# A hybrid decoder step: where the sums of x are formed, which slots the state tiles use, and whose queue loads the first merged values

## The chip, the cores and the metric

The kernel runs on one core of a Trainium2 chip. The metric is the device time of one execution in microseconds (us); less is better. The core's engines work side by side and meet at semaphores: TensorE (PE in the profile; PEld is its weight load), VectorE (DVE), ScalarE (ACT), GpSimd (POOL) and SyncE (SP, which here only issues DMAs). Each engine takes its own instructions in order. An instruction that waits holds up all that stand behind it on its engine, and the same goes for DMA issues on a queue.

## What is computed

One layer of a decoder for 2048 prompt tokens and 64 sample tokens (8 sequences of 8), model width 1024. Cut to what matters:

```python
z = x @ w_in                                   # q, k, v, gates of both branches
o_att = swa(q, k, v, sink, rel_bias)           # sliding window attention, with a relative bias
o_gla, S = gla(gq, gk, gv, log_a, s0)          # gated linear attention, 4 heads, state S carried on
h_att = (o_att * silu(g_att)) @ w_pa
h_gla = (norm(o_gla) * silu(g_gla)) @ w_pg
merged = sigmoid(r_att) * h_att + sigmoid(r_gla) * h_gla
y = merged @ w_o
x = layer_norm(ALPHA * x + y, ln_g, ln_b)
```

The recurrent state of the samples (`s0`) is read, advanced and written back as an output.

## The kernel before

**Stages.** The program runs in four stages: attention (to about 350 us of the span), GLA head by head (352 to 1080 us, each head six chunks of 384, 384, 384, 384, 256 and 320 tokens), the merge passes (four products, `w_pa`, `w_ra`, `w_rg`, `w_pg`, in 84 units; to 1660 us), and the output projection with the layer norm (to the end).

**Split values.** Every fp32 operand of a matmul is split in a high and a low part: ACT casts the high part (`CAST`, L112) and DVE, sometimes POOL, subtracts it (L113). A product is three matmuls: high by high, high by low, low by high (L182 to L184, L195 to L197, L1218 to L1220). So PE waits for an ACT cast and then a DVE or POOL subtraction of each new operand.

**Sums of x.** The merge passes use a scheme with seven products in place of eight: it multiplies sums and differences of blocks of the operands. `combine_x` forms four such values from two 128x704 rows of x, by four `tensor_tensor` of 128x352 on POOL (L855 to L858), loads the two rows on SP's queue (L853), and stores each result with a DMA of its own, also on SP's queue (L860). A list of 30 sums waits to be done: 6 of the attention's output (`ua_d` to `ac_d`), 12 of the input (`xT` to `xc_d`), 12 of the GLA's output (`ug_d` to `uc_d`). In GLA two of them are done at the start of each of the chunks 0, 1 and 2 of a head, 24 in all; six are left for the merge passes.

**Pools.** `wtile` gives a 128x1024 slot of a pool of 28. The weights' parts, the values `gv`, the rows x1 and x2 of the sums, the bias of the attention and `S0`, the samples' state, all turn in these slots, and the pools of the next stage lie in the same memory. At the end of a head `samp_b` advances `S0` (L836) and writes it out (L838, `o_ss<-S`): on SP, but in the last head on POOL's queue.

**Order.** PE's instructions are written out by hand. The other engines' order is made by a scheduler. `tc.issue_after(...)` holds an instruction of another engine behind a named one.

**Out of the merge stage.** `merge_sink` (L1096) forms merged values on DVE and SP stores them (`mg_d<-a`, L1099). `load_m` loads the first eight 128x384 tiles of them back (`xst<-mg_d`, L1168), ACT and DVE split them (`x`), and the projection's first matmuls (L195 to L197 with `woh`, `wol`) use them.

Of the kernel before, what the change touches and what calls it, by code (L numbers as in the profile page):

```python
# [21 lines left out]
P = 128  # L22
D = 1024
# [28 lines left out]
def kernel(ctx, tc, io):  # L52
# [19 lines left out]
    def wtile(dt=F32, name="w"):  # L72
        return sb.tile([P, D], dt, tag="w", name=name, bufs=28)

# [144 lines left out]

    st, hi, lo = sb.tile([P, D], F32, tag="wst", name="wst", bufs=2), wtile(F32R, "wh"), wtile(F32R, "wl")
# [88 lines left out]
    def setup2():  # L311
        flat = bs_d.rearrange("h q j -> h (q j)")
        for kv in range(2):
            b = wtile(name="bias").rearrange("p (g k) -> p g k", g=G)
            for g in range(G):
                f = flat[kv * G + g, 127:127 + P * (LB - 1)].rearrange("(q j) -> q j", j=LB - 1)
                nc.gpsimd.dma_start(b[:, g, :], f[:, :2 * W])
            st1["bias", kv] = b
# [470 lines left out]
    def samp_a(B):  # L789
# [20 lines left out]
        for bh in (0, 4):  # L810
            S0 = wtile(name="S0").rearrange("p (b v) -> p b v", b=4)
            nc.sync.dma_start(S0, io["state"][bh:bh + 4, B["h"]].rearrange("b k v -> k b v"))
            B["S0", bh] = S0
# [33 lines left out]

    def combine_x(new):
        src, dst, kh, k, s = combos.popleft()
        ts = slice(2 * s * MT, 2 * (s + 1) * MT)  # L850
        x1, x2 = new("x1")[:, :2 * MT], new("x2")[:, :2 * MT]
        for x_, k_ in ((x1, k), (x2, kh + k)):
            nc.sync.dma_start(x_, ug_d[k_ // 2][:, k_ % 2, ts] if src is None else src[:, k_, ts])  # L853
        t0, t1 = slice(0, MT), slice(MT, 2 * MT)
        nc.gpsimd.tensor_tensor(x2[:, t1], x2[:, t1], x1[:, t1], ALU.subtract)  # L855
        nc.gpsimd.tensor_tensor(x1[:, t1], x1[:, t1], x1[:, t0], ALU.subtract)
        nc.gpsimd.tensor_tensor(x1[:, t0], x1[:, t0], x2[:, t1], ALU.add)
        nc.gpsimd.tensor_tensor(x2[:, t0], x1[:, t0], x2[:, t0], ALU.subtract)  # L858
        for n_, x_, t in ((0, x1, t1), (1, x1, t0), (2, x2, t1), (3, x2, t0)):
            nc.sync.dma_start(dst[n_, :, s, k], x_[:, t])  # L860

# [22 lines left out]
    for h in range(GH):  # L884
        W2 = {}
        wcap(16 + 6 * h)
        for c, (t0, T) in enumerate(CHUNKS):
# [12 lines left out]
            gla_z(B)  # L900
            if c < 3:
                for _ in range(2):
                    combine_x(lambda n: wtile(name=n))
            wv = [wt2("v", 0), wt2("v", 1)]
# [24 lines left out]
            proj(ps[:, :T], wt2("k"), x, T)  # L929
            gla_k(B, ps[:, :T])  # L930
            if len(CHUNKS) - 4 < c < len(CHUNKS) - 1:
                wload()
# [7 lines left out]
            gla_q(B, ps[:, :T])  # L940
            tick()
            if end:
                chain(B)
# [43 lines left out]
    class Pass:  # L987
# [31 lines left out]
        def raw_x(self, i, s):  # L1019
# [7 lines left out]
            else:  # L1027
                d = [self.kept[{7: 2, 6: 1, 5: 0, 4: 3}[i]][:, s, :self.kh]]
            n = self.kh // len(d)
# [132 lines left out]

    def load_m(t, u, n, last=False):

        out = []
        for k in range(KT):
            st = ox.tile([P, TM], F32, tag="xst", name="xst", bufs=8)
            nc.sync.dma_start(st[:, :n + 32 * last], mg_d[t][:, k, u:u + n + 32 * last])  # L1168
            if last:
# [22 lines left out]
    for n, (q, i, s) in enumerate(units):  # L1192
        if n >= 2 * len(ORDER) * MS and n % 3 == 0 and combos:
            with tc.issue_after(pin["x"].ins), tc.issue_after(pin["p"].ins):
                combine_x(lambda t: mtile("xc", 2 * T, 5))
        if n >= 3 * len(ORDER) * MS and n % 4 == 0 and len(wo) < 4:
# [29 lines left out]
        if n == len(units) - 2:  # L1226

            xf, x, xr0 = load_m(1, 0, TM), [], []
    phase.close()
# [195 lines left out]
```

## Time and profile before

| what | value |
|---|---|
| median of 3 runs | 1871.84 us (1870.64 to 1873.26) |
| the profiled execution, its time | 1869.53 us |
| its span, first to last instruction | 1867.8 us |
| PE busy | 1818.6 us (97%) |
| DVE busy | 1252.3 us (67%) |
| ACT busy | 850.9 us (46%) |
| POOL busy | 513.0 us (27%) |
| mean granted TensorE clock | 0.988 |

The table is read from the top: an engine that is busy for 97% of the span is the bound, and the time that it isn't busy, 49.2 us, is what others make it wait for. A granted clock of 1.00 is 2.4 GHz; the other level is 1.2 GHz, and a mean between them says which part of a stretch ran at which. Time at the lower level counts as busy, so it does not show in PE's share.

### The profile page before, as it was taken

How to read it: one execution, taken by the hardware profiler on the slowest of the kernel's cores; microseconds unless marked ns; L12 is line 12 of the kernel's file. 1: busy time of each engine (PE TensorE's matmuls, PEld its weight loads, DVE VectorE, ACT ScalarE, POOL GpSimd, SP SyncE). 2: the span in 40 equal slices, each digit the busy share in tenths (PEclk: the TensorE clock that was granted, in tenths of full speed). 3: DMA queues.
4: the chain of work that ended last, by engine and by line, in shares of the span. 5: the costliest groups of instructions: out<-in, count | busy, mean ns of one | idle time of the engine just before them, and what ended most of it. 6: DMA issues, size and time to landing. Idle time of an engine off the chain costs nothing.

```text
span 1867.8 us, 32468 instructions
## 1 busy us (share of the span) xinstructions
PE 1818.6 (97%) x11683; PEld 1727.2 (92%) x11683; DVE 1252.3 (67%) x2566; ACT 850.9 (46%) x1947; POOL 513.0 (27%) x655
## 2 busy tenths in 40 slices
PE   8999999999999999999999989999999999999997
PEld 7989898899999999999999979999999999987886
DVE  6686688755675666657665659758656666956655
ACT  5444455545664664556455543444543543221110
POOL 3310111412134114211421124421255153631111
PEclk9999999999999999999999989999999999999999
DMA  7111003533365237514642179868887866895531
GB/s 240 53 55 38 27 32 123 178 129 104 108 212 182 81 104 234 178 57 140 203 134 73 42 248 313 278 200 275 292 318 259 299 217 244 282 310 187 157 117 40
DMA packets 200513, 315.84 MB, mean 169 GB/s; under 512 B 22413, under 2 KB 162149, under 8 KB 200336
## 3 DMA queue, kind: packets, MB, share of 16 engines
q1 hardware_dynamic: 194736, 306.19, 49.8%
q0 software_dynamic: 5616, 7.58, 1.5%
q8 instruction: 92, 1.51, 0.3%
q14 instruction: 69, 0.57, 0.1%
HBM read 228.52 MB, written 86.14 MB: 168 GB/s over the span
## 4 chain that ended last, share of the span: by engine, by line
PE 42%; DVE 4%; DMA 3%; POOL 2%; issue 1%; ACT 1%; SPq 0%; DVEq 0%; POOLq 0%; ACTq 0%
PE pa L1219 8%; PE pa L1218 8%; PE pa L1220 8%; PE pd L196 4%; PE pd L197 4%; PE pd L195 4%; PE pd L183 2%; PE pd L184 2%; PE pd L182 2%; DMA cs<-tt_d 1%; DVE xl L113 1%; DVE wl L113 0%; DVE fin L1096 0%; PE pa L750 0%; PE pa L751 0%
## 5 line engine op out<-in xcount | busy, mean ns | idle before, releaser
L182 PE MATMUL pd<-x,wh 128*128 128x384 f32 (+2 forms) x1248 | 410.5, 329 | 6.1 <-ACT x L112 5.9
L183 PE MATMUL pd<-x,wh 128*128 128x384 f32 (+2 forms) x1248 | 405.3, 325 | 0.4 <-POOL x L113 0.2
L184 PE MATMUL pd<-x,wl 128*128 128x384 f32 (+2 forms) x1248 | 404.7, 324 | 0.6 <-DVE wl L113 0.6
L1219 PE MATMUL pa<-xl,wh 128*128 128x352 f32 x1176 | 380.1, 323 | 9.8 <-DVE xl L113 9.4
L1218 PE MATMUL pa<-xh,wh 128*128 128x352 f32 x1176 | 381.7, 325 | 0.3 <-ACT wh L112 0.3
L1220 PE MATMUL pa<-xh,wl 128*128 128x352 f32 x1176 | 379.5, 323 | 0.0
L182 PEld LDWEIGHTS pd<-x,wh 128*128 128x128 f32 x1248 | 237.5, 190 | 16.0 <-issue 8.9
L183 PEld LDWEIGHTS pd<-x,wh 128*128 128x128 f32 x1248 | 237.5, 190 | 1.5 <-DVE x L113 1.1
L184 PEld LDWEIGHTS pd<-x,wl 128*128 128x128 f32 x1248 | 237.3, 190 | 1.0 <-DVE wl L113 1.0
L1219 PEld LDWEIGHTS pa<-xl,wh 128*128 128x128 f32 x1176 | 222.9, 190 | 12.4 <-DVE xl L113 12.4
L1218 PEld LDWEIGHTS pa<-xh,wh 128*128 128x128 f32 x1176 | 222.0, 189 | 1.1 <-ACT wh L112 0.4
L1220 PEld LDWEIGHTS pa<-xh,wl 128*128 128x128 f32 x1176 | 222.0, 189 | 0.0
L113 DVE TENSOR_TENSOR xl<-xs,xh 128x1408 fp32r<-128x1408 f32 x63 | 111.8, 1774 | 68.5 <-ACT xh L112 67.5
L195 PE MATMUL pd<-wh,x 128*128 128x256 f32 x512 | 149.6, 292 | 2.9 <-ACT x L112 2.7
L196 PE MATMUL pd<-wh,x 128*128 128x256 f32 x512 | 147.7, 289 | 2.7 <-DVE x L113 1.9
L197 PE MATMUL pd<-wl,x 128*128 128x256 f32 x512 | 145.7, 285 | 0.0
L112 ACT CAST x<-xst 128x384 fp32r<-128x384 f32 (+2 forms) x164 | 78.5, 485 | 140.2 <-PE pd L196 117.5
L112 ACT CAST xh<-xs 128x1408 fp32r<-128x1408 f32 x63 | 86.6, 1374 | 100.9 <-PE pa L1220 75.7
L742 POOL TENSOR_SCALAR sq<-sq 128x1 f32<-128x1 f32 (+1 forms) x68 | 18.3, 269 | 366.4 <-ACT ring L741 366.3
L195 PE MATMUL pd<-woh,x 128*128 128x512 f32 x256 | 102.6, 401 | 3.7 <-ACT x L112 3.7
L196 PEld LDWEIGHTS pd<-wh,x 128*128 128x128 f32 x512 | 98.9, 193 | 6.2 <-DVE x L113 5.7
L197 PE MATMUL pd<-wol,x 128*128 128x512 f32 x256 | 102.5, 400 | 0.6 <-DVE wol L113 0.6
(318 smaller groups left out, 3755.2 us busy)
## 6 DMA issues: line engine op xcount, KB each, us to landing
wst<-wt SPq DMA_DIRECT2D x33, 512.0 KB, 3.6
xs<-xc_d SPq DMA_DIRECT2D x24, 704.0 KB, 5.3
cs<-tt_d SPq DMA_DIRECT2D x48, 352.0 KB, 4.9
u<-xT SPq DMA_DIRECT2D x84, 192.0 KB, 3.8
xst<-xT SPq DMA_DIRECT2D x76, 192.0 KB, 2.7
xs<-xT SPq DMA_DIRECT2D x18, 704.0 KB, 6.1
ws<-w_ra SPq DMA_DIRECT2D x36, 256.0 KB, 4.3
ws<-w_rg SPq DMA_DIRECT2D x36, 256.0 KB, 4.6
```

The costliest lines, as they stand in the source:

```text
L112: pin["a"] = nc.scalar.copy(dst_h, src)
L113: i = eng.tensor_tensor(dst_l, src, dst_h.bitcast(F32), ALU.subtract)
L182: mm(ps, hi[:, s], xh[:, :T], start=(k == 0), stop=False)
L183: mm(ps, hi[:, s], xl[:, :T], start=False, stop=False)
L184: mm(ps, lo[:, s], xh[:, :T], start=False, stop=(k == n - 1))
L195: mm(ps, xh[:, xs], hi, start=(k == 0), stop=False)
L196: mm(ps, xl[:, xs], hi, start=False, stop=False)
L197: mm(ps, xh[:, xs], lo, start=False, stop=(k == KT - 1))
L742: nc.gpsimd.tensor_scalar(sq[:n], sq[:n], EPS, None, op0=ALU.add)
L1218: mm(ps, wh[:, ks], xh[:, ts], start=(k == 0), stop=False)
L1219: mm(ps, wh[:, ks], xl[:, ts], start=False, stop=False)
L1220: mm(ps, wl[:, ks], xh[:, ts], start=False, stop=(k == q.kh - 1))
```

## The change

The change has three parts.

1. **Slots.** The pool of 128x1024 slots has 26 in place of 28. Two slots of their own, with tag "s", lie at the bottom of the pool (`stile("first")` takes the place before anything else). The attention's bias and GLA's `S0` use them.
2. **Sums.** `combine_x` becomes `combine_load` and `combine_do`. In GLA the loads are written at the start of the chunk, and the four operations go to DVE: one sum behind `gla_k`, one behind `gla_q`, each held behind the instruction in `pin["d"]`. The chunks are 1, 2 and 3 of a head, not 0, 1 and 2. In the merge passes the operations stay on POOL. The four results are stored with two DMAs, not four, in another order of n, and the list of which result is kept where follows that.
3. **Queue.** The first `load_m` issues its eight loads on ACT's queue, not on SP's.

```diff
-        return sb.tile([P, D], dt, tag="w", name=name, bufs=28)
+        return sb.tile([P, D], dt, tag="w", name=name, bufs=26)
+    def stile(name):
+        return sb.tile([P, D], F32, tag="s", name=name, bufs=2)
...
+    stile("first")
...
-            b = wtile(name="bias").rearrange("p (g k) -> p g k", g=G)
+            b = stile("bias").rearrange("p (g k) -> p g k", g=G)
...
-            S0 = wtile(name="S0").rearrange("p (b v) -> p b v", b=4)
+            S0 = stile("S0").rearrange("p (b v) -> p b v", b=4)
...
-    def combine_x(new):
+    def combine_load(new):
         src, dst, kh, k, s = combos.popleft()
         ts = slice(2 * s * MT, 2 * (s + 1) * MT)
         x1, x2 = new("x1")[:, :2 * MT], new("x2")[:, :2 * MT]
         for x_, k_ in ((x1, k), (x2, kh + k)):
             nc.sync.dma_start(x_, ug_d[k_ // 2][:, k_ % 2, ts] if src is None else src[:, k_, ts])
+        return x1, x2, dst[:, :, s, k]
+
+    def combine_do(x1, x2, dst, eng):
+
         t0, t1 = slice(0, MT), slice(MT, 2 * MT)
-        nc.gpsimd.tensor_tensor(x2[:, t1], x2[:, t1], x1[:, t1], ALU.subtract)
-        nc.gpsimd.tensor_tensor(x1[:, t1], x1[:, t1], x1[:, t0], ALU.subtract)
-        nc.gpsimd.tensor_tensor(x1[:, t0], x1[:, t0], x2[:, t1], ALU.add)
-        nc.gpsimd.tensor_tensor(x2[:, t0], x1[:, t0], x2[:, t0], ALU.subtract)
-        for n_, x_, t in ((0, x1, t1), (1, x1, t0), (2, x2, t1), (3, x2, t0)):
-            nc.sync.dma_start(dst[n_, :, s, k], x_[:, t])
+        eng.tensor_tensor(x2[:, t1], x2[:, t1], x1[:, t1], ALU.subtract)
+        eng.tensor_tensor(x1[:, t1], x1[:, t1], x1[:, t0], ALU.subtract)
+        eng.tensor_tensor(x1[:, t0], x1[:, t0], x2[:, t1], ALU.add)
+        eng.tensor_tensor(x2[:, t0], x1[:, t0], x2[:, t0], ALU.subtract)
+        for n_, x_ in ((0, x1), (2, x2)):
+            nc.sync.dma_start(dst[n_:n_ + 2].rearrange("n p t -> p n t"), x_.rearrange("p (n t) -> p n t", n=2))
...
             gla_z(B)
-            if c < 3:
-                for _ in range(2):
-                    combine_x(lambda n: wtile(name=n))
+            sums = [combine_load(lambda n: wtile(name=n)) for _ in range(2 if c in (1, 2, 3) else 0)]
+
+            def combine():
+                if sums:
+                    with tc.issue_after(pin["d"].ins):
+                        combine_do(*sums.pop(0), nc.vector)
...
             gla_k(B, ps[:, :T])
+            combine()
...
             gla_q(B, ps[:, :T])
             tick()
+            combine()
...
-    def load_m(t, u, n, last=False):
+    def load_m(t, u, n, last=False, queue=nc.sync):
...
-            nc.sync.dma_start(st[:, :n + 32 * last], mg_d[t][:, k, u:u + n + 32 * last])
+            queue.dma_start(st[:, :n + 32 * last], mg_d[t][:, k, u:u + n + 32 * last])
...
-                combine_x(lambda t: mtile("xc", 2 * T, 5))
+                combine_do(*combine_load(lambda t: mtile("xc", 2 * T, 5)), nc.gpsimd)
...
-            xf, x, xr0 = load_m(1, 0, TM), [], []
+            xf, x, xr0 = load_m(1, 0, TM, queue=nc.scalar), [], []
```

PE's order is the same before and after. On the other engines the scheduler's order moves, at these three places above all.

On ACT, where the attention's last blocks overlap GLA's first chunk: `em`, `ek`, `dm` and `gb` are GLA's exponentials, `pT` is the transposed probabilities that PE's L417 waits for. Before:

```order
L386 ACTIVATE s,sm<-s,nm 128x256 x4
L388 ACTIVATE es<-es 128x4
L701 ACTIVATE em<-dm 128x384
L702 ACTIVATE ek<-ek 128x384
L703 ACTIVATE dm<-dm 128x384
L704 ACTIVATE gb<-gb 128x384
L112 CAST gv<-pd 128x256
L406 COPY pT<-pa 128x512
```

After:

```order
L390 ACTIVATE s,sm<-s,nm 128x256 x4
L392 ACTIVATE es<-es 128x4
L410 COPY pT<-pa 128x512
L705 ACTIVATE em<-dm 128x384
L706 ACTIVATE ek<-ek 128x384
L707 ACTIVATE dm<-dm 128x384
L708 ACTIVATE gb<-gb 128x384
L115 CAST gv<-pd 128x256
```

The copy of `pT` has moved from behind the four exponentials to ahead of them.

On DVE, in chunk 1 of the first head, from the parts of `ak` to the gates. Before:

```order
L113 TENSOR_TENSOR ak<-pa,ak 128x128
L715 TENSOR_TENSOR em<-pd,em 128x384
L715 TENSOR_TENSOR ek<-pd,ek 128x384
L767 SCALAR_TENSOR_TENSOR ring<-ring,e_4734,pa 128x256
L113 TENSOR_TENSOR st<-ring,st 128x256
```

After:

```order
L116 TENSOR_TENSOR ak<-pa,ak 128x128
L863 TENSOR_TENSOR x_5140<-x_5140,x_5139 128x352
L864 TENSOR_TENSOR x_5139<-x_5139 128x352
L865 TENSOR_TENSOR x_5139<-x_5139,x_5140 128x352
L866 TENSOR_TENSOR x_5140<-x_5139,x_5140 128x352
L719 TENSOR_TENSOR em<-pd,em 128x384
L719 TENSOR_TENSOR ek<-pd,ek 128x384
```

A sum of four instructions stands ahead of `em`; the chunk's second sum stands in the same way between a `st` and the `sg` of L784.

On SP's queue, in the first two chunks of the first head (`ua_d<-sil` stores the attention's last output, `u<-xT` loads the next chunk's x). Before:

```order
L853 DMA x_4749<-ua_d 128x704
L860 DMA ac_d<-x_4737 128x352
L860 DMA ac_d<-x_4736 128x352 x2
L860 DMA ac_d<-x_4737 128x352
L860 DMA ac_d<-x_4749 128x352
L860 DMA ac_d<-x_4748 128x352 x2
L860 DMA ac_d<-x_4749 128x352
L424 DMA ua_d<-sil 128x320 x4
L147 DMA u<-xT 128x384 x4
```

After:

```order
L857 DMA x_4718<-ua_d 128x704
L150 DMA u<-xT 128x384 x2
L428 DMA ua_d<-sil 128x320 x4
L150 DMA u<-xT 128x384 x2
L857 DMA x_5139<-ua_d 128x704
L857 DMA x_5140<-ua_d 128x704
L857 DMA x_5143<-ua_d 128x704
L868 DMA ac_d<-x_4713 128x2x352
```

The loads of x have moved from behind the sums' eight stores to ahead of them, and the next chunk's sums are loaded before this chunk's are stored.

At the end of the merge stage ACT's order now has the eight loads of `load_m` as two groups of four: one ahead of the last unit's `xh` (the high part of its operand), one behind it, and the eight casts `x<-xst` behind that.

## Rows read from the trace of the kernel before

**Rows 1.** PE's waits over the whole span: what waited for what, us in total, times, the longest.

```profile
PE pa L1219 <- DVE xl L113: 9.4, 5, 6.2
PE pd L195 <- ACT x L112: 6.5, 4, 3.7
```

**Rows 2.** Windows of the span (from:to, its length, then busy us of each engine, the granted clock, the DMA share and GB/s).

```profile
355.00:372.00 17.00, 13.70 (x73) 9.99 (x73) 14.77 (x27) 10.28 (x28) 9.93 (x10) 0.80 0.55 179
405.00:435.00 30.00, 27.46 (x168) 26.67 (x168) 11.72 (x31) 9.03 (x28) 17.32 (x22) 0.94 0.59 200
540.00:555.00 15.00, 13.81 (x104) 12.75 (x103) 11.66 (x24) 10.07 (x24) 4.59 (x6) 1.00 0.69 217
...
700.00:735.00 35.00, 33.08 (x228) 31.82 (x227) 26.08 (x68) 20.85 (x55) 11.06 (x15) 0.95 0.73 239
735.00:880.00 145.00, 144.96 (x1040) 143.00 (x1040) 91.37 (x231) 83.44 (x201) 33.98 (x60) 1.00 0.40 126
880.00:905.00 25.00, 23.47 (x170) 22.41 (x170) 17.84 (x39) 13.34 (x33) 10.38 (x13) 1.00 0.60 195
...
1064.00:1092.00 28.00, 19.50 (x122) 16.80 (x121) 15.63 (x50) 10.07 (x32) 7.29 (x15) 0.82 0.60 198
...
1655.00:1690.00 35.00, 30.62 (x130) 24.53 (x129) 18.67 (x31) 9.01 (x14) 6.75 (x8) 0.90 0.89 303
```

**Rows 3.** PE in order of time, where attention gives way to GLA (start, us, instruction, count, idle time before it and what ended that).

```profile
363.24 1.08 PE L417 MATMUL pa<-pT,vt 128*64 128x512 f32 x4 [1.42 <-ACT pT L406]
365.94 1.97 PE L417 MATMUL pa<-pT,vt 128*64 128x512 f32 x2 [1.62 <-DVE pT L404]
...
371.95 0.34 PE L197 MATMUL pd<-wl,x 128*128 128x256 f32 x1
```

**Rows 4.** ACT there: the copy behind the four exponentials (L701 to L704).

```profile
362.60 0.58 ACT L406 COPY pT<-pa 128x512 f32<-128x512 f32 x1
```

**Rows 5.** DVE in order of time there.

```profile
362.11 3.17 DVE L392 TENSOR_SCALAR s<-s,rd 128x256 f32<-128x256 f32 x4
365.20 0.68 DVE L404 COPY pT<-pa 128x512 f32<-128x512 f32 x1
```

**Rows 6.** POOL in order of time there: the first and the last of eight instructions of sums, back to back.

```profile
355.51 0.93 POOL L855 TENSOR_TENSOR x<-x,x 128x352 f32<-128x352 f32 x1
...
363.95 0.93 POOL L858 TENSOR_TENSOR x<-x,x 128x352 f32<-128x352 f32 x1
```

**Rows 7.** PE's longest wait in the second chunk of the first head.

```profile
421.61 0.39 PE L749 MATMUL pa<-st,qih 128*128 128x256 f32 x1 [2.26 <-ACT st L112]
```

**Rows 8.** ACT in order of time there.

```profile
418.20 1.00 ACT L112 CAST x<-u 128x384 fp32r<-128x384 f32 x2 [5.39 <-DMA u<-xT]
```

**Rows 9.** SP's queue there (start, time of the issues together, count).

```profile
403.87 7.42 SPq L860 DMA_DIRECT2D ac_d<-x  x8
411.38 1.86 SPq L424 DMA_DIRECT2D ua_d<-sil  x4
413.35 2.04 SPq L147 DMA_DIRECT2D u<-xT  x4
```

**Rows 10.** POOL there: the last of eight instructions of sums, back to back from 402.88.

```profile
409.99 0.95 POOL L858 TENSOR_TENSOR x<-x,x 128x352 f32<-128x352 f32 x1
```

**Rows 11.** PE in order of time where the merge passes begin.

```profile
1087.31 0.66 PE L1219 MATMUL pa<-xl,wh 128*128 128x352 f32 x1 [6.15 <-DVE xl L113]
...
1092.41 0.32 PE L1218 MATMUL pa<-xh,wh 128*128 128x352 f32 x1
```

**Rows 12.** DVE in order of time there.

```profile
1080.74 0.99 DVE L780 SCALAR_TENSOR_TENSOR sg<-pa,nw_h,sg 128x128 f32<-128x128 f32 x4
1086.36 0.89 DVE L113 TENSOR_TENSOR xl<-xc,xh 128x704 fp32r<-128x704 f32 x1 [4.63 <-DMA o_ss<-S]
```

**Rows 13.** POOL's last issue of the samples' state there.

```profile
1081.13 0.76 POOL L838 DMA_DIRECT2D o_ss<-S  x1 [1.09 <-DVE S L836]
```

**Rows 14.** PE where the output projection begins.

```profile
1664.01 0.80 PE L195 MATMUL pd<-woh,x 128*128 128x512 f32 x1 [3.74 <-ACT x L112]
...
1669.04 0.43 PE L197 MATMUL pd<-wol,x 128*128 128x512 f32 x1
```

**Rows 15.** SP's queue there.

```profile
1659.01 4.07 SPq L1168 DMA_DIRECT2D xst<-mg_d  x8
```

**Rows 16.** ACT there.

```profile
1649.43 1.37 ACT L112 CAST xh<-xs 128x1408 fp32r<-128x1408 f32 x1 [8.19 <-DMA xs<-uc_d]
1663.44 4.16 ACT L112 CAST x<-xst 128x384 fp32r<-128x384 f32 x8 [12.64 <-DMA xst<-mg_d]
```

**Rows 17.** Groups of instructions by line and shape: count, busy us, mean ns of one, idle time before them. A 128x352 operation on POOL and on DVE.

```profile
L855 POOL TENSOR_TENSOR x<-x,x 128x352 f32<-128x352 f32 x24 | 23.4, 975 | 54.3 <-DMA x<-ua_d 46.5 <-DMA x<-xT 4.9 <-DMA x<-ug_d 2.9
...
L1078 DVE TENSOR_TENSOR a<-a,pa 128x352 f32<-128x352 f32 x48 | 23.8, 515 | 5.9 <-PE pa L1220 5.8
```

**Rows 18.** DVE in order of time in the third chunk of the second head, a chunk in which PE waits for nothing.

```profile
624.33 0.56 DVE L715 TENSOR_TENSOR em<-pd,em 128x384 f32<-128x384 f32 x1 [1.63 <-PE pd L184]
...
626.22 0.43 DVE L113 TENSOR_TENSOR st<-ring,st 128x256 fp32r<-128x256 f32 x1 [0.47 <-ACT st L112]
...
635.24 0.61 DVE L780 SCALAR_TENSOR_TENSOR sg<-pa,nw_h,sg 128x128 f32<-128x128 f32 x2 [1.51 <-PE pa L777]
...
639.96 0.56 DVE L218 SCALAR_TENSOR_TENSOR sg<-th,pd 128x384 f32<-128x384 f32 x1 [1.15 <-ACT th L217]
```

More of the change, by code (lines that the diff above doesn't have):

```diff
@@ L1027, in raw_x @@
             else:
-                d = [self.kept[{7: 2, 6: 1, 5: 0, 4: 3}[i]][:, s, :self.kh]]
+                d = [self.kept[{6: 0, 5: 1, 4: 2, 7: 3}[i]][:, s, :self.kh]]
             n = self.kh // len(d)
```

## The prediction

> **What bounds the kernel now.** PE does. It is busy for 1818.6 of 1867.8 us, its instructions and their order stay as they are, so the change can only give back time in which PE waits or runs at the lower clock, or add to it. I read PE's waits first [rows 1]: the two longest entries are DVE's xl (9.4 us, one of them 6.2) and ACT's x (6.5 us, one of 3.7), a single stall each at a stage's border. Then I cut the span into windows [rows 2]. Undisturbed GLA loses nothing (144.96 busy of 145 us), so the losses sit in a few windows, and for each I read in order of time which engine came last. The other thing to see in a window is the granted clock: 0.80, 0.82, 0.90 and 0.94 mean that after the stall PE ran on at 1.2 GHz for some us. That loss is no idle time and comes on top.
>
> **The change part by part.** All times are of the profiled execution (1869.53 us, its span 1867.8), which is 2.31 us below the median of the runs shown; the sum is made on it, and the 2.31 is added at the end.
>
> (a) 355 to 372 us, attention into GLA: idle 17.00 - 13.70 = 3.3 us [rows 2]. PE waits 1.42 us for ACT's pT and 1.62 for DVE's, and then runs at half speed until 371.95 [rows 3]: from 365.94 that is 6.0 us, half of it lost, 3.0. At stake: 6.3. ACT's copy at 362.60 stands behind four exponentials of GLA [rows 4]. DVE's copy at 365.20 stands behind an L392 group that took 3.17 us [rows 5], all while POOL does eight instructions of sums from 355.51 to 364.88 [rows 6]. After the change no sum is done in chunk 0, and on ACT pT stands ahead of the exponentials. I take 5.0. Ends: 2.0 (ACT's wait and a part of the clock's loss) and 6.3.
>
> (b) 405 to 435, second chunk of the first head: idle 30.00 - 27.46 = 2.54, clock 0.94 of 30 us = 1.8 more [rows 2], 4.3 together. PE's 2.26 us for st [rows 7] go back to ACT, which sat 5.39 us for the load u<-xT [rows 8]. SP issued it at 413.35, behind eight stores of sums, 7.42 us [rows 9], that waited for POOL's sums, the last at 409.99 [rows 10]. Now the loads stand ahead of the stores, and there are four stores, not eight. I take all 4.3; ends 2.5 (the idle alone) and 4.3.
>
> (c, d, e) The other heads' starts: idle 15.00 - 13.81 = 1.2 at 540, 35.00 - 33.08 = 1.9 and 0.05 of 35 = 1.75 of clock at 700, 25.00 - 23.47 = 1.5 at 880 [rows 2]. All have sums of chunk 0 on POOL in the window, with their loads and stores on SP. These move to the chunks 1 to 3. 6.4 at stake. I take all of it; the low end is 1.9, if only the idle at 700 goes.
>
> (f) 1064 to 1092, the first merge unit. PE waits 6.15 us for xl and then runs at half speed until 1092.41 [rows 11], 5.1 us, of which 2.55 are lost. DVE had been free since 1081.73 and waited 4.63 us for the DMA o_ss<-S [rows 12], which POOL issued at 1081.13 [rows 13]: the xl tile lies where an S0 tile lay. With S0 in slots of its own, xl needs only its operand and its cast. DVE's sg (L780) then ends at 1081.73, and xl takes 0.89, so PE goes on at about 1082.6, 4.7 us earlier. I take 5.0, as a shorter stall should also leave some of the clock. Ends: 4.4, and 7.0 if PE never falls to the lower clock. DVE's next late partner would be a weight's part (wl) in a slot of the last stores, one unit later and off the path.
>
> (g) 1655 to 1690, the output projection: idle 35.00 - 30.62 = 4.38 [rows 2], with the half speed from 1664.01 to 1669.04 [rows 14], 2.5, in all 6.9. ACT's casts of x wait 12.64 us and end at 1667.6 [rows 16]; SP issues the loads only at 1659.01, in 4.07 us [rows 15], as they stand behind the last units' stores and loads on its queue. On ACT's queue they have no such neighbours: ACT sat idle 8.19 us ahead of the last xh [rows 16], so four loads go out in that gap and four right behind that cast, at 1650.8 to 1652.9. From issue to the first cast it took 1663.44 - 1659.01 = 4.4 us, so the last four can be cast from 1657.3, 0.52 each, and end at 1659.4, before PE asks at 1664.01 - 3.74 = 1660.27. I take 6.0, since waits for wol stay. Ends: 3.0 and 6.9.
>
> (h) Added on DVE: 24 sums of four 128x352 operations. On POOL one took 975 ns, on DVE the same shape takes 515 [rows 17], though there with one operand in PSUM: 4 x 0.515 = 2.06 us a sum, 24 x 2.06 = 49 us. DVE in a chunk of GLA is 63% busy (91.37 of 145) [rows 2]. In a chunk in which PE waits for nothing the gaps are [rows 18]: 1.63 us ahead of em, where the first sum goes, and 1.51 ahead of sg, where the second goes. Each is short by some 0.5 us (0.43 and 0.55). The next gaps, 0.47 ahead of st and 1.15 ahead of the second gate, take that up. So the cover is DVE's own idle time; without it the cost is 12 x 0.98 = 11.8 us. The range is 0 to 11.8. I take 3.0, near the lower end, because rows 18 are of a chunk that gets sums now.
>
> What costs nothing: POOL loses 96 operations, 96 x 0.975 = 94 us of work, which nobody asks for. S0's loads stand earlier on SP and wait there for the state's store; what stands behind them is x of the chunk after, wanted much later. The pool of 26 slots lost exactly the two that S0 or the bias took.
>
> Sum: 5.0 + 4.3 + 6.4 + 5.0 + 6.0 = 26.7, less 3.0 = 23.7. 1869.5 - 23.7 = 1845.8, and with 2.3, **1848.1 us**. By all high ends (30.9, nothing added) 1840.9; by all low ends (13.8 gained, 11.8 added) 1869.8.
>
> At (g) a rule speaks against my 6.0. The row shows 4.07 us of issue on SP and a last cast 7.3 us after PE asked for the first. The Trainium skill, "DMA: Bandwidth & Descriptors", section "Issuing engines are not separate DMA queues", says that DMAs from several engines run on the same 16 DMA engines and that spreading them saves only the issuing sequencer's time. By it (g) would be worth 4.1 at most, and the sum 1850. I keep 6.0, since what I count is that the loads leave SP's queue position, not that they run faster.
>
> **The rivals.**
>
> *The stalls come back in another coat.* At each head's start other things lie close behind: the cast of st, the ring on POOL's sq, the subtraction of x. If half of (a) to (g) returns, the gain is 13.4, less 3 = 10.4: 1861.5. For it: rows 2 show several small waits in each window. Against: the sums are the common part of all of them.
>
> *Only the issue time is saved at (g)*, by waits of ACT's queue for the last stores of merged values: 4.1 less what ACT's last xh loses behind four issues (4.07 / 2 = 2.0). Then 1852. For it: ACT works in order. Against: 8.19 us of idle time there.
>
> *The sums on DVE cost more than the stalls (slower).* DVE works in order. If a sum's row of x has not landed, or a sum is longer than its gap, everything behind it waits: em, the state's parts, the gate, the next chunk's x, and then PE. The point from which it decides: 26.7 / 24 = 1.1 us of PE's time for each sum. At 2.06, a whole sum on the path, it is 49.4 - 26.7 = 22.7 slower: 1895. For it: SP is in order too, one load of a pair has a slot that is free late, and the sums stand ahead of em. Against: the loads stand a chunk ahead of their sums, and rows 18 have gaps nearly as long as the sums.
>
> *The change doesn't do what it says*, as xl or pT waits for something as late as before: (f) or (a) alone is 5 us of the 23.7, so this ends between the first rival and the forecast, or within 0.2% if both fail and the sums cost their upper end.
>
> **How the numbers follow.** My forecast 0.62, half returned 0.17, issue time only 0.09, slower by DVE 0.07, nothing left of the gain 0.05. Faster by over 0.2% (3.7 us, about what a measurement of this kernel tells from no change) is the first three, 0.88; same 0.05; slower 0.07. The range 1840 to 1862 takes in the high ends and the first two rivals, and leaves out the last two cases and some of the error in the sum: 0.18.
>
> **What would show it.** In the trace of the changed kernel PE's wait for xl at the first merge unit should be under 2 us and ACT's x at the projection under 1. The windows at the five GLA starts should have a clock of 0.95 or more and idle times under 1 us, but for the first. DVE should have 49 us more, POOL 94 less, and PE's list of waits should have no new line at em, st, sg or x within chunks 1 to 3; such lines, 24 times over, would make the prediction wrong on the slow side. If xl is late again, look for what holds its tile.

## The result, and the profile after

The changed kernel takes 1844.84 us (median of 4 runs, 1843.05 to 1846.22) against 1871.24 (4 runs, 1866.16 to 1873.26): ratio 0.9862, 95% interval 0.984 to 0.9885, so 26.4 us less by the medians. The forecast was 1848.1 with 23.7 less on the trace; the two profiled executions differ by 23.3 (1869.53 and 1846.22).

PE's waits over the whole span, to be held against [rows 1]:

```profile
PE pa L1233 <- DVE xl L116: 7.6, 5, 2.6
PE pd L185 <- ACT x L115: 6.3, 3, 4.9
PE pa L1232 <- ACT xh L115: 2.3, 1, 2.3
PE pa L421 <- DVE pT L408: 1.1, 1, 1.1
```

ACT's x at the projection (L195 before, L198 now) has left the list. L185 was there before too, 5.9 us with a longest of 4.7: it is the start of the program. The longest wait for xl fell from 6.2 to 2.6 us, and a new line has come: xh, 2.3 us once.

The windows that answer to [rows 2] (same columns; each place lies earlier by what was won ahead of it):

```profile
350.00:370.00 20.00, 18.93 (x145) 17.00 (x145) 16.95 (x45) 18.10 (x52) 3.89 (x4) 1.00 0.46 141
394.00:426.00 32.00, 32.00 (x272) 31.68 (x271) 21.07 (x55) 16.44 (x41) 3.20 (x7) 1.00 0.61 206
527.00:545.00 18.00, 18.00 (x140) 17.59 (x140) 12.05 (x40) 13.12 (x34) 2.05 (x4) 1.00 0.56 168
685.00:720.00 35.00, 35.00 (x262) 34.59 (x261) 26.00 (x75) 23.30 (x59) 5.65 (x10) 1.00 0.54 166
715.00:860.00 145.00, 144.96 (x1039) 143.00 (x1038) 103.41 (x266) 83.13 (x202) 20.11 (x44) 1.00 0.47 150
860.00:890.00 30.00, 30.00 (x226) 29.61 (x225) 21.18 (x62) 20.72 (x56) 2.95 (x7) 1.00 0.46 137
1045.00:1075.00 30.00, 26.24 (x160) 23.53 (x160) 18.71 (x53) 13.43 (x42) 9.95 (x17) 0.89 0.63 207
1615.00:1655.00 40.00, 35.15 (x183) 32.42 (x183) 26.61 (x40) 7.31 (x12) 15.30 (x14) 0.91 0.95 314
```

GLA is clean. In its first window 1.07 us of idle time are left, at the other heads' starts and in the second chunk of the first head nothing, and PE has the full clock in all of them. The undisturbed 145 us took 12 us more of DVE (103.41 for 91.37) and lost PE nothing: 144.96 busy as before. The two borders of the merge stage still have idle time and the lower clock.

PE's instructions and their order are the same in all kernels here, so the trace of one can be laid on that of before, matmul by matmul. The table has the change of that distance over each stretch, in us (less is a gain; letters as in the prediction, start to 350 us of before, (a) to 400, (b) to 535, (c, d, e) to 1070, (f) to 1093, the merge passes to 1600, (g) to 1750). The names are those of the experiments below.

```
                   start     a      b   c,d,e    f    merge    g    total
changed kernel       1.8   -6.3   -5.6   -8.9   -4.4    0.8   -0.7  -23.3
the same, again     -0.3   -7.1   -5.6   -8.9   -5.4   -0.5   -1.5  -29.3
e1_loads_on_sp      -0.4   -7.0   -5.6   -8.9   -5.5   -1.2    0.1  -28.5
e2_loads_late        0.3   -7.1   -5.6   -8.9   -5.3    5.5   -1.4  -22.5
e3_sums_on_pool      0.5   -7.1   -5.4   -8.9   -5.2    5.5   -0.6  -21.2
e4_sums_doubled     -0.7   -7.1   -4.7   -7.2   -5.2    2.3   -2.4  -25.1
e5_only_queue        1.3    0.0    0.1   -1.1    0.8    1.6   -0.1    2.8
e6_only_slots        0.8   -2.0    0.5   11.0   -5.3    4.7   -1.9    7.9
e7_no_slots          1.5   -6.9   -5.6   -8.9    0.7   -1.5    2.8  -17.8
e8_chunks_0_2        1.5   -5.7   -5.6   -8.9   -5.5   -0.1   -0.2  -24.4
e9_wo_first          1.5   -7.1   -5.6   -8.9   -5.2   -2.2   -4.7  -32.3
e9 again (e12)       1.4   -7.1   -5.6   -8.9   -5.2   -0.5   -2.5  -28.4
e10_only_chunks      0.6   -6.3    1.0   -8.9   -2.0    4.7    2.1   -8.8
```

The columns (b) to (e) repeat within a few tenths wherever a kernel has the same parts; (a) and (f) differ by 0.8 and 1.0 between the two traces of the changed kernel itself. The start and the merge column do not repeat: they move by 2 and by 8 us between executions of kernels that are the same there. Nor does (g): kernels whose code is the same there differ in it by 2 us and more. Part of that is taken up at the end, and it is why single places tell more here than the total.

At (a), ACT in order of time:

```profile
362.45 0.57 ACT L410 COPY pT<-pa 128x512 f32<-128x512 f32 x1
362.91 0.52 ACT L705 ACTIVATE em<-dm 128x384 f32<-128x384 f32 x1
```

The copy now runs ahead of the exponentials, and PE waits for no pT there. DVE's side has changed too. Its L392 group, which [rows 5] show at 3.17 us while POOL did sums, took 1.14 us in the same trace at 349.94, before POOL's sums began. In the changed kernel, where POOL does no sums, it takes 1.13:

```profile
363.79 1.13 DVE L396 TENSOR_SCALAR s<-s,rd 128x256 f32<-128x256 f32 x4
```

The sums on DVE, in the third chunk of the second head (DVE in order of time):

```profile
610.27 0.28 DVE L116 TENSOR_TENSOR ak<-pa,ak 128x128 fp32r<-128x128 f32 x1
610.47 0.52 DVE L863 TENSOR_TENSOR x<-x,x 128x352 f32<-128x352 f32 x1
...
612.14 0.53 DVE L866 TENSOR_TENSOR x<-x,x 128x352 f32<-128x352 f32 x1
612.58 0.55 DVE L719 TENSOR_TENSOR em<-pd,em 128x384 f32<-128x384 f32 x1
...
614.46 0.43 DVE L116 TENSOR_TENSOR st<-ring,st 128x256 fp32r<-128x256 f32 x1 [0.47 <-ACT st L115]
```

Where [rows 18] had 1.63 us of idle time ahead of em there is a sum, and em follows it at once. The idle 0.47 us ahead of st are still there, so DVE was not even late for it. Over the whole span DVE is busy for 28.6 us more (1280.9 for 1252.3), not for the 49 of the forecast: the sums take 50.2, but DVE's other instructions, the same in number, take less time than before, as the L392 group at (a) does.

At (f), DVE in order of time:

```profile
1061.70 0.99 DVE L784 SCALAR_TENSOR_TENSOR sg<-pa,nw_h,sg 128x128 f32<-128x128 f32 x4
1062.61 0.88 DVE L116 TENSOR_TENSOR xl<-xc,xh 128x704 fp32r<-128x704 f32 x1
```

xl follows sg without a gap ([rows 12] had 4.63 us), and PE waits 1.43 us for it in place of 6.15.

```profile
1063.54 0.66 PE L1233 MATMUL pa<-xl,wh 128*128 128x352 f32 x1 [1.43 <-DVE xl L116]
```

At (g), first ACT with its queue, then SP's queue, then PE:

```profile
1618.48 1.37 ACT L115 CAST xh<-xs 128x1408 fp32r<-128x1408 f32 x1 [10.88 <-DMA xs<-uc_d]
1621.29 2.42 ACTq L1182 DMA_DIRECT2D xst<-mg_d  x4
1630.22 1.36 ACT L115 CAST xh<-xs 128x1408 fp32r<-128x1408 f32 x1 [10.37 <-DMA xst<-mg_d]
```

```profile
1622.75 0.38 SPq L1045 DMA_DIRECT2D xs<-uc_d  x1
```

```profile
1631.64 0.43 PE L1232 MATMUL pa<-xh,wh 128*128 128x352 f32 x1 [2.29 <-ACT xh L115]
1634.63 0.66 PE L1233 MATMUL pa<-xl,wh 128*128 128x352 f32 x1 [2.56 <-DVE xl L116]
...
1639.20 0.39 PE L1233 MATMUL pa<-xl,wh 128*128 128x352 f32 x1
```

The stall has moved, not gone. The last unit waits 2.29 us for xh and 2.56 for xl and runs at half speed until 1639.20; the projection behind it then finds its x ready. The cast of xh at 1630.22 names an xst load as its releaser, but ACT's four issues had ended at 1623.71. What landed at that time is xs, the last unit's own operand, issued at 1622.75 and 7.4 us under way. That transfer took 5.2 us before. In all seven traces in which four loads of the merged values are issued into it, it took 6.1 to 7.4 us; in all seven in which they are not (before, e1, e2, e6, e9, e10, e12), 4.2 to 5.2. Issues with the time to landing, of the changed kernel, then of e2, where no xst load is under way beside it:

```profile
xs<-uc_d SPq DMA_DIRECT2D x1, 704.0 KB, 7.4
```

```profile
xs<-uc_d SPq DMA_DIRECT2D x1, 704.0 KB, 4.6
```

### The profile page after: what moved, and what is told of

Same layout as the page of the kernel before. It is cut to its first block, busy times and chain, and to the rows that moved or that the text cites. A ratio compares the mean times of both kernels' runs of the same rounds, so it can differ in the third digit from the quotient of the medians.

```text
span 1844.4 us, 32399 instructions
## 1 busy us (share of the span) xinstructions
PE 1807.9 (98%) x11683; PEld 1722.2 (93%) x11683; DVE 1280.9 (69%) x2662; ACT 849.9 (46%) x1947; POOL 422.3 (23%) x559
## 4 chain that ended last, share of the span: by engine, by line
PE 91%; DVE 3%; DMA 3%; issue 1%; POOL 1%; SPq 0%; ACT 0%; DVEq 0%; ACTq 0%; POOLq 0%
PE pd L185 11%; PE pd L187 11%; PE pd L186 11%; PE pa L1234 9%; PE pa L1233 9%; PE pa L1232 9%; PE pd L199 7%; PE pd L198 7%; PE pd L200 7%; PE pa L421 2%; DMA cs<-tt_d 1%; PE pa L406 1%; PE pa L755 1%; PE pa L753 1%; PE pa L754 1%
## 5 line engine op out<-in xcount | busy, mean ns | idle before, releaser
L185 PE MATMUL pd<-x,wh 128*128 128x384 f32 (+2 forms) x1248 | 409.1, 328 | 7.0 <-ACT x L115 6.3
L185 PEld LDWEIGHTS pd<-x,wh 128*128 128x128 f32 x1248 | 236.5, 190 | 17.2 <-issue 8.9
L198 PE MATMUL pd<-wh,x 128*128 128x256 f32 x512 | 147.9, 289 | 0.0
L199 PE MATMUL pd<-wh,x 128*128 128x256 f32 x512 | 145.6, 284 | 1.2 <-DVE x L116 1.1
L199 PE MATMUL pd<-woh,x 128*128 128x512 f32 x256 | 101.5, 396 | 0.0
L198 PE MATMUL pd<-woh,x 128*128 128x512 f32 x256 | 101.5, 396 | 0.0
```

What stands on the lines that cost most here:

```text
L185: mm(ps, hi[:, s], xh[:, :T], start=(k == 0), stop=False)
L198: mm(ps, xh[:, xs], hi, start=(k == 0), stop=False)
L199: mm(ps, xl[:, xs], hi, start=False, stop=False)
```

## The experiments

The theory after the result: the place of the sums in the program made the stalls in GLA, the slots made the one at (f), and the queue gave nothing, since its loads now collide with the last unit's. The rivals: the engine made the stalls in GLA (POOL against DVE); the queue is worth what was forecast and the traced run was unlucky; the slots work in GLA too.

**e1_loads_on_sp: the changed kernel without the third part.**

```diff
-            xf, x, xr0 = load_m(1, 0, TM, queue=nc.scalar), [], []
+            xf, x, xr0 = load_m(1, 0, TM), [], []
```

> The changed kernel with its third part undone: the first eight loads of merged values are issued on SP's queue again. In the trace of the changed kernel the stall at the projection is gone, but the last merge unit now waits 2.29 us for xh and 2.56 for xl and runs at half clock, so that matched by its matmuls the border gave back only 0.4 us of the 6.0 forecast. Theory (the queue moved the stall and did not remove it): within 3 us of the changed kernel's 1844.8, with PE waiting some 3.7 us for ACT's x at the projection and no wait for xh at the last unit. Rival (the prediction's 6.0 us stand and the traced run was unlucky): 1849 to 1852.

Measured: 1846.08 us (1841.12 to 1848.67), ratio to before 0.9853 (0.9832 to 0.9875), the same as with the part. PE's waits have the old line at the projection, and none for xh:

```profile
PE pd L198 <- ACT x L115: 4.0, 1, 4.0
```

The last unit's xl is late here too, with no load on ACT's queue beside it, so its wait is not all the queue's doing:

```profile
1624.93 0.43 PE L1233 MATMUL pa<-xl,wh 128*128 128x352 f32 x1 [1.91 <-DVE xl L116]
```

The rival of the prediction's full 6.0 us falls: (g) has 0.1 in the table, and e5, with the part alone, is no faster than the kernel before.

**e5_only_queue: the kernel before with the third part alone** (`load_m` gets the argument `queue`, and the first call passes ACT's).

> The kernel before with the third part alone: the first eight loads of merged values on ACT's queue. Theory (the border's stall only moves, from x at the projection to xh at the last unit): the same as the kernel before within 2 us. Rival (the prediction's 6.0 us, masked in the changed kernel by something else that it does): 5 to 7 us faster.

Measured: 1873.67 us, ratio 1.0012 (0.9995 to 1.0029). By itself the queue gives nothing either. PE waits for xh at the last unit as in the changed kernel:

```profile
PE pa L1218 <- ACT xh L112: 1.9, 1, 1.9
```

**e2_loads_late: all eight loads on ACT's queue, behind the last cast of xh.**

```diff
-        if n == len(units) - 2:
-
-            xf, x, xr0 = load_m(1, 0, TM, queue=nc.scalar), [], []
...
+        if n == len(units) - 1:
+            with tc.issue_after(pin["a"].ins):
+                xf, x, xr0 = load_m(1, 0, TM, queue=nc.scalar), [], []
```

> The changed kernel with all eight loads on ACT's queue, but held behind the last unit's cast of xh. Theory (four loads of 192 KB ahead of that cast share the DMA engines with the last unit's 704 KB load, which took 7.4 us to land against 5.1 before): no wait for xh at the last unit, the loads land within the last unit's 7.6 us, and the time is 1837 to 1841. Rival (the loads are simply too late now): PE waits for x at the projection by 2 to 4 us and falls to half clock: 1843 to 1848.

Measured: 1847.49 us (1846.39 to 1851.72), ratio 0.9868 (0.9851 to 0.9885). The mechanism is as expected, but for a wait of 1.52 us for the last unit's xl: no wait for xh, none for x at the projection, full clock, and xs lands in 4.6 us. The time is not; it lies in the range of the rival, though by another wait than the rival named: 20 us into the projection PE waits for w_o.

```profile
1662.54 0.50 PE L198 MATMUL pd<-woh,x 128*128 128x512 f32 x1 [2.20 <-ACT woh L115]
1663.80 0.51 PE L200 MATMUL pd<-wol,x 128*128 128x512 f32 x1 [0.52 <-DVE wol L116]
```

SP issued those rows of w_o behind eight loads of the second x:

```profile
1649.70 6.75 SPq L1182 DMA_DIRECT2D xst<-mg_d  x8
1656.54 2.75 SPq L1153 DMA_DIRECT2D wst<-w_o  x2
```

And in the merge passes this execution lost 5.5 us by the pace of its matmuls, which the edit does not touch.

**e3_sums_on_pool: the changed kernel with its sums on POOL, in the same places.**

```diff
-                        combine_do(*sums.pop(0), nc.vector)
+                        combine_do(*sums.pop(0), nc.gpsimd)
```

> The changed kernel with the sums of GLA in chunks 1 to 3, in the same place of the program, but on POOL. Theory (what stalled PE at a head's start was the place of the sums in chunk 0, with their loads and stores ahead of x on SP; the engine matters little): 1844 to 1849, DVE 49 us less busy, no stall at 355 to 372 or at a head's start. Rival (the engine decides: POOL's sums lie ahead of sq and slow DVE by half wherever they stand): half of the 19 us that GLA gave back is lost: 1852 to 1862, with waits of ACT's ring for POOL's sq.

Measured: 1848.6 us, ratio 0.9868 (0.9851 to 0.9886). From (a) to (e) it gives back what the changed kernel does. The whole of GLA, first in this kernel, then in the changed one:

```profile
340.00:1050.00 710.00, 709.52 (x5200) 697.16 (x5200) 459.47 (x1204) 409.61 (x1023) 189.18 (x302) 1.00 0.43 138
```

```profile
340.00:1050.00 710.00, 708.76 (x5196) 696.54 (x5195) 501.01 (x1295) 412.09 (x1024) 95.97 (x207) 1.00 0.44 138
```

POOL has 93 us more, DVE 42 less, and PE is idle for 0.5 and 1.2 us of 710. Moved like this, to the chunks 1 to 3 and behind the chunk's own work, the sums cost PE the same on either engine, though ACT's ring waits for POOL's sq by up to 5.3 us, and by 1.6 at most in the changed kernel; the rival falls for these places. What sums on POOL do in chunk 0, where the kernel before has them, is not tested by it. That is taken up under e8.

**e4_sums_doubled: four more operations on DVE ahead of each sum in GLA.**

```diff
+        if eng is nc.vector:
+            for f in (f1, f2, f1, f2):
+                eng.tensor_tensor(f[:, 2 * MT:], x1[:, :D - 2 * MT], x2[:, :D - 2 * MT], ALU.add)
```

> The changed kernel with four more tensor_tensor of 128x320 on DVE ahead of each sum in GLA, whose results go to the unused end of the sum's own tiles: the cost of a sum on DVE about doubled, 96 operations or some 46 us more. Theory (DVE's idle time covers the sums with room to spare, since GLA lost nothing to them): 1844 to 1850. Rival (the gaps are just full: 1.63 and 1.51 us for sums of 2 us): each further us of a sum reaches PE, 24 x 1.9 = 46 at most, half of it likely: 1865 to 1890.

Measured: 1849.4 us (1844.41 to 1853.04), ratio 0.9881 (0.9861 to 0.9901). GLA's share of that is read from the table: 40 us more on DVE cost 0.9 at (b) and 1.7 at (c, d, e).

```profile
L866 DVE TENSOR_TENSOR x<-x,x 128x320 f32<-128x320 f32 x96 | 40.5, 483 | 0.0
```

So the sums of the change sit well inside DVE's idle time; with as much again per sum the first 2.6 us in all reach PE.

**e6_only_slots: the kernel before with the first part alone** (26 slots, `stile` for the bias and S0).

> The kernel before with the first part alone: 26 slots, and two slots of their own for the bias and S0. Theory (xl no longer waits for the store of S0): PE's wait for xl at the first merge unit 1.4 instead of 6.2 us, 4 to 6 us faster at that place, and GLA as before with its stalls; two slots fewer for the sums on POOL may cost up to 2. Rival (the 4.7 us came from the freer queues of SP and POOL, not from the slots): 0 to 1 us.

Measured: 1882.01 us, the median of 12 runs of which two took 2262.69 and 6283.74; 1878.78 without those two, ratio 1.005 (1.0031 to 1.007): slower. (f) gains 5.3, as expected, and (c, d, e) lose 11.0, where up to 2 were expected. (a) gains 2.0, which was not followed up. With two slots fewer, the sums at a head's start get theirs late. SP's queue at the second head:

```profile
533.84 0.33 SPq L858 DMA_DIRECT2D x<-xT  x1
536.63 2.38 SPq L865 DMA_DIRECT2D xc_d<-x  x4
539.06 0.45 SPq L858 DMA_DIRECT2D x<-xT  x1
...
548.94 1.90 SPq L150 DMA_DIRECT2D xst<-xT  x4
```

The last of the sums' rows is loaded at 539.06, where before all four went out together from 528.96. Its sum starts on POOL at 543.42, and ACT's ring (GLA's output, normed) waits for sq (the norm's scale, formed on POOL) behind that sum's first operations, then PE for x behind the ring:

```profile
546.24 0.47 ACT L749 ACTIVATE ring<-pa,sq 128x256 f32<-128x256 f32 x1 [5.34 <-POOL sq L748]
```

```profile
547.16 0.58 PE L198 MATMUL pd<-wh,x 128*128 128x256 f32 x1 [2.89 <-ACT x L115]
```

**e7_no_slots: the changed kernel without the first part** (28 slots, `wtile` for the bias and S0).

> The changed kernel with its first part undone: 28 slots, and the bias and S0 among them. Theory: xl waits some 6 us for o_ss<-S again, 4 to 6 us slower than the changed kernel at that place (ratio to before 0.989 instead of 0.986), and GLA without its stalls as in the changed kernel. Rival (the slots matter in GLA too, as the rows of the sums then take turns with S0): new waits for x or S0 at the end of a head as well, 8 us or more slower.

Measured: 1852.05 us, ratio 0.9896 (0.9876 to 0.9915). GLA is as in the changed kernel, (f) gives nothing (it loses 0.7), and PE's wait for xl is back:

```profile
PE pa L1229 <- DVE xl L113: 12.9, 5, 6.6
```

**e8_chunks_0_2: the changed kernel with its sums in the chunks 0 to 2.**

```diff
-            sums = [combine_load(lambda n: wtile(name=n)) for _ in range(2 if c in (1, 2, 3) else 0)]
+            sums = [combine_load(lambda n: wtile(name=n)) for _ in range(2 if c in (0, 1, 2) else 0)]
```

> The changed kernel with the sums on DVE behind gla_k and gla_q, but in the chunks 0, 1 and 2 of a head as in the kernel before. With the sums on POOL in chunks 1 to 3 GLA ran as in the changed kernel, so the engine did not decide. Theory (what decides is that no sum, with its loads and stores on SP, falls into the first chunk of a head and the end of the one before): half or more of the 19 to 21 us that GLA gave back is lost: ratio to before 0.992 to 0.998. Rival (what decides is the place within the chunk, behind gla_k and gla_q, so that the loads of x go ahead of the sums' stores on SP): no more than 4 us lost, ratio 0.986 to 0.989.

Measured: 1848.11 us, ratio 0.9874 (0.9858 to 0.989). (b) to (e) are as in the changed kernel and (a) 0.6 to 1.4 short of it. My theory that only the chunk decides falls; the rival, the place within the chunk, fits. But in chunk 0 this kernel also has its sums on DVE; no run has POOL's sums in chunk 0 behind `gla_k`, so there the place is not told apart from the engine. The traces speak for the engine. At (a), ACT's copy is behind the four exponentials again, as in the kernel before, yet PE waits 0.20 us for it and not 1.42; DVE, which feeds the exponentials, is not held up (its L396 group takes 1.14 us):

```profile
363.03 0.58 ACT L410 COPY pT<-pa 128x512 f32<-128x512 f32 x1
```

```profile
363.66 1.93 PE L421 MATMUL pa<-pT,vt 128*64 128x512 f32 x6 [0.20 <-ACT pT L410]
```

At a head's start ACT's ring needs POOL's sq, and the cast of the next x stands behind the ring. In the kernel before, sq stood behind POOL's sums, and the ring waited 3.08, 4.07 and 3.41 us for it at the three starts; in e8, e3, e10 and the changed kernel it waits 1.05 at each. The second head, before, then changed:

```profile
544.64 0.47 ACT L744 ACTIVATE ring<-pa,sq 128x256 f32<-128x256 f32 x1 [3.08 <-POOL sq L743]
```

```profile
532.48 0.47 ACT L748 ACTIVATE ring<-pa,sq 128x256 f32<-128x256 f32 x1 [1.05 <-POOL sq L747]
```

**e10_only_chunks: the kernel before, one line.**

```diff
-            if c < 3:
+            if c in (1, 2, 3):
                 for _ in range(2):
                     combine_x(lambda n: wtile(name=n))
```

> The kernel before with one line changed: two whole sums (loads, POOL, four stores each) at the start of the chunks 1, 2 and 3 of a head, not 0, 1 and 2. Theory (the chunk decides): the stalls at 355 to 372 and at the three heads' starts go, some 16 us faster, and the stall in the second chunk of the first head, where sums still stand ahead of x on SP, stays: ratio 0.990 to 0.993. Rival (the place within the chunk decides): stalls of the same size one chunk later, ratio 0.997 to 1.002.

Measured: 1857.84 us, ratio 0.9922 (0.9906 to 0.9937). It gives (a), 6.3, and (c, d, e), 8.9, and leaves (b), where the sums' stores still stand ahead of x on SP. Together with e8 and e3: moving the sums to a later chunk clears the heads' starts, and so does leaving them in chunk 0 but on DVE behind `gla_k` and `gla_q`; (b) is clear in every kernel with the place behind `gla_k` and `gla_q`. Those kernels also have half as many stores, which no run takes apart from the place.

(f) gives 2.0 without the slots. Here another tile waits for the samples' state, xh and not xl:

```profile
1070.93 0.78 ACT L112 CAST xh<-xc 128x704 fp32r<-128x704 f32 x1 [4.84 <-DMA o_ss<-S]
```

**e9_wo_first, and e11 and e12: a version past the changed kernel.** e2, with the last two rows of w_o on POOL's queue and their casts ahead of the second x:

```diff
-        pin["o"] = nc.sync.dma_start(st, io["w_o"][i])
+        pin["o"] = (nc.gpsimd if i > 5 else nc.sync).dma_start(st, io["w_o"][i])
...
-                x = rest_m(*order[j + 1], last=(j + 2 == len(order)))
+                with tc.issue_after(last_wo.ins) if j == 0 else nullcontext():
+                    x = rest_m(*order[j + 1], last=(j + 2 == len(order)))
```

> The kernel of e2, with the last two rows of w_o loaded on POOL's queue and their casts ahead of the second x on ACT. In e2 the border between the merge and the projection was free of stalls (PE waited for nothing and kept the full clock), and 20 us later PE waited 2.20 us for woh and 1.3 us more for wol, as SP had issued w_o's last two rows behind eight loads of merged values that took 6.75 us to issue. Theory (the wait moved on to w_o, and w_o is the last one there): no wait above 0.6 us from 1600 us to the end, 3.5 us less than e2 and some 7 less than the changed kernel from the last unit to the end. Rival (another wait comes next, for the second x or for xr): 1 us or less.

Measured: 1839.86 us (1837.42 to 1841.0), ratio 0.9825 (0.9804 to 0.9847). At (g) the trace gives 4.7 us over before, 4.0 more than the changed kernel. From 1600 us on the trace shows one wait of PE, 1.85 us for the last unit's xl, where no wait above 0.6 was expected. So it was run again beside the changed kernel.

> The changed kernel once more, beside the next run on the same chip: ratio to before 0.985 to 0.988, 1842 to 1848 us.

> The kernel of e9 once more, beside the changed kernel: 5 to 9 us below it, by the border between merge and projection, which has no stall here; all else as in the changed kernel, but for the pace of the matmuls in the merge stage, which differs from run to run by up to 1.4%.

Measured: the changed kernel 1844.39 us (1840.23 to 1846.98), ratio 0.985 (0.9834 to 0.9866); e9's kernel 1842.98 (1841.3 to 1847.46), ratio 0.9848 (0.9832 to 0.9865). The 5 to 9 us did not come back. In that execution PE waited again for w_o:

```profile
PE pd L198 <- ACT woh L115: 0.9, 1, 0.9
PE pd L200 <- DVE wol L116: 0.9, 2, 0.5
```

Its trace gives 2.5 us at (g), the changed kernel's second trace 1.5. e4, whose code at this border is the changed kernel's, has 2.4 there. A gain over the changed kernel is not established, by the times or by the traces.

## Why the prediction came out right, point by point

The time lay 3.3 us below the forecast and well within the range, but the terms of the sum did not all hold; their errors cancelled, and that the total came so close is luck.

- **(a)** 5.0 was forecast; 6.3 and 7.1 came in two traces, the whole stake. The order on ACT was read rightly, but it is not what most of the gain hangs on: e8 has the old order and gains 5.7. The part on POOL's side, that its sums hold up DVE, fits the traces: the L392 group ahead of DVE's pT took 3.17 us beside POOL's sums and 1.13 to 1.14 without them.
- **(b)** 4.3 forecast, 5.6 measured. The chain by way of SP's stores fits: e10, which keeps the stores ahead of x, keeps the stall.
- **(c, d, e)** 6.4 forecast, 8.9 measured. The sums of chunk 0 were rightly named; the link is POOL's sq, late behind them (e8), which the prediction has only in its first rival. The three starts gave 2.0, 4.5 and 2.4 us, each 0.8 to 0.9 more than the idle time and the clock of its window. The forecast counted too little: back to back these matmuls start 0.12 us apart, but each is on record for 0.28, so the idle time before a late one begins only when the one ahead is off the record. Two successive ones at the second head, before and after:

```profile
545.57 0.39 PE L195 MATMUL pd<-wh,x 128*128 128x256 f32 x1 [0.63 <-ACT x L112]
546.16 0.38 PE L196 MATMUL pd<-wh,x 128*128 128x256 f32 x1 [0.20 <-DVE x L113]
```

```profile
534.64 0.28 PE L198 MATMUL pd<-wh,x 128*128 128x256 f32 x1
534.76 0.28 PE L199 MATMUL pd<-wh,x 128*128 128x256 f32 x1
```

  The second starts 0.59 us behind the first and not 0.12, a loss of 0.47 of which 0.20 counts as idle; the first loses more in the same way. Summed over that start, PE lost 2.0 us and its idle time is 1.2.
- **(f)** 5.0 forecast, 4.4 and 5.4 measured. S0's slot was the cause: alone (e6) it gives 5.3, and without it (e7) nothing is left; e10, without it too, gains 2.0 where xh in place of xl waits for the same store. What I costed at nothing here, the two slots lost, is free only because the sums moved too. In e6 it costs 11.0.
- **(g)** 6.0 forecast, 0.7 and 1.5 measured, and not told apart from no gain: against the kernel before, kernels without this part take 0.1 more (e1), 1.9 less (e6) and 2.1 more (e10) there. This is the step that failed. The forecast took the loads' landing time from a stretch in which nothing of the last unit was still to come, and named ACT's idle time as their cover. That cover was a wait for the last unit's own 704 KB, and four loads of 192 KB issued into it made that transfer take 7.4 us, not 5.2. The last unit's xl, late by 1.91 us in e1 as well, adds to the stall for a reason that was not looked for. The rival "only the issue time" was near, by another way: ACT's cast was late, but not behind the issues. The rule that I weighed and set aside, in the Trainium skill's "DMA: Bandwidth & Descriptors", section "Issuing engines are not separate DMA queues", says that transfers of all queues interleave on the same 16 engines; the 7.4 against 5.2 and 4.6 us here agree with it. By it I gave (g) 4.1 at most, and it measured less.
- **(h)** 3.0 forecast for the sums on DVE, nothing measured: 144.96 of 145 us, and e4 shows room for nearly as much again. Their cost on DVE, 4 x 0.52 us a sum by the trace, was forecast at 4 x 0.515. The rival that the sums cost more than the stalls had its place right (ahead of em and sg) and its condition never occurred. The sign that DVE would have 49 us more was missed (28.6), by what POOL's sums had cost DVE before.

Taken together: (g) was 5 us too high, (a) to (e) some 5 too low and (h) 3 too high, and in the traced execution the start and the pace of the merge passes took 2.6 that no term held. That is why the total fits so well.

## What to carry to other kernels

An idle engine is no cover for a load when what it waits for is another load: ask what is still in flight, since the early transfer is paid for by the one that is needed first. Where work off the critical path stalls the bound engine, ask what the bound engine needs from that side at that moment: here the sums stalled PE on POOL in a head's first chunk, not on POOL in later chunks behind the chunk's own work, and not on DVE in either. And two edits can be worth a gain together and a loss apart, as the slots here, so each part's price holds only for the buffers that the others leave.

## What was not expected of the hardware

In the merge stage PE's matmuls (128x352, new weights for each) keep one of three paces, 158.9, 160.0 or 161.1 ns from start to start, for hundreds of us, without idle time and at the full clock, and change it only where PE has stalled. The mean over 84 successive matmuls, at some times of the span:

```
                  at 1190   1300   1400   1470    after 1550
before             158.9   158.9   158.9   158.9   161.1
changed kernel     160.0   160.0   160.0   160.0   160.0
the same, again    158.9   158.9   158.9   158.9   158.9
e2_loads_late      161.1   161.1   161.1   161.1   160.0
e3_sums_on_pool    161.1   161.1   161.1   161.1   158.9
e4_sums_doubled    158.9   158.9   158.9   158.9   160.0
e6_only_slots      158.9   158.9   160.0   160.0   158.9
e10_only_chunks    161.1   161.1   161.1   161.1   160.0
```

The same kernel has it one way in one execution and another way in the next. From 1160 to 1500 us of before a step is worth 2.4 us, two steps 4.8; this is most of the merge column where the pace is 161.1 (5.5, 5.5 and 4.7 for e2, e3 and e10). It does not explain the rest of that column: e4 loses 2.3 at the pace of before, and e6's 4.7 holds a stall near 1380. Of the 6.0 us between the two traces of the changed kernel the merge column has 1.3; 2.1 lie in the start, the other 2.6 at (a), (f) and (g). GLA and the projection keep one pace in all of them. What sets it at a stall was not tried.
